# Down projections of two squared-ReLU MLPs as Strassen's seven products, with TensorE's instructions of both MLPs in source order

## The chip, the cores and the metric

The kernel runs on one core of one Trainium2 chip. The metric is the device time of one launch in microseconds; the time before is 1177.26 us, the median of three runs (1177.13 to 1177.45). A profile is one further execution, recorded by the hardware profiler. The engines are PE (TensorE: matmuls; PEld is its weight load), DVE (VectorE), ACT (ScalarE), POOL (GpSimd) and SP (which only issues transfers). ACT and SP issue the transfers from HBM on queues of their own. Each engine works through its instructions in order and waits on semaphores for the others.

## The reference

One inference step of a two-layer streaming encoder on 512 new and 64 running tokens, all in float32 (T = 576, model width D = 1024, inner width 4 D).

```
for i in range(2):
    x = x + mixer_i(rmsnorm(x, norm_mix[i]))      # 0: pooling mixer, 1: indexed sparse attention
    h = rmsnorm(x, norm_mlp[i])
    u = relu(h @ w_up[i])                         # 1024 -> 4096
    x = x + (u * u) @ w_down[i]                   # 4096 -> 1024
y = rmsnorm(x, norm_final)
```

The mixers also return new states (keys, values, indexer keys, the last 15 rows). The two MLPs hold most of the arithmetic: each has an up and a down product of 576 x 1024 x 4096.

## The kernel before, in words

The residual stream lies transposed in SBUF: eight feature tiles `x[k]` of 128 partitions by 576 tokens, two to a buffer. A float32 product is made from three matmuls in the fast float32 format: a value v is split into an upper part (ACT casts it) and a lower part (v less the upper part, a DVE subtraction), and upper x upper, upper x lower and lower x upper are summed in PSUM. `project` (L151 to L162) does this for one 128-wide output tile: eight k tiles, three passes, two halves of 288 tokens in two PSUM banks, so 48 matmuls.

Weights come in blocks of 128 x 1024 floats (512 KB): one output tile with its eight k tiles. `next_block` (L135) loads the next block by a transfer on ACT's queue, casts it on ACT (L115), subtracts on DVE (L116; on POOL at a few places) and keeps two blocks ahead. There are two raw buffers and three buffers each for the upper and lower parts.

`mlp` (L245) works in four chunks of 1024 inner features. A chunk is eight up products (`up`), each followed by relu and the factor 1/rms on DVE (L252), a square on ACT (L253) and a split into u (L145, L146); then eight down products (`dn`), each over the eight u tiles of the chunk and added into x[m] by DVE (L277). `xs` are the normalised inputs, split once; `Norm` sums squares of x, and `stats` and `spread` turn them into 1/rms on PE, ACT and DVE (the tiles `st` and `rb`). The first up product runs before 1/rms is known. The last three down products of layer 1 are made in two parts of the tokens by `last`, together with the final norm.

The order on each engine is set by a scheduler that goes by priorities and estimated times; it may move instructions of one stage between those of another. Only `last` holds PE to the source order, by `tc.manual_schedule`. All stages share the same pools of SBUF buffers; the MLPs borrow the tags of the attention for u and xs. PSUM has three slots of two banks (`ps`) and two of one bank (`po`).

Of the kernel before, what the change touches and what calls it, by code (L numbers as in the profile page):

```python
# [16 lines left out]
P = 128  # L17
# [19 lines left out]
SLOTS = {"x": 4, "xs": 8, "a": 3, "b": 3, "c": 3, "d": 3, "e": 2}  # L37
# [3 lines left out]
def pool_dsa_kernel(ctx: ExitStack, tc: tile.TileContext, a, o):  # L41
# [4 lines left out]
    slots = ctx.enter_context(tc.tile_pool(name="slots", bufs=1))  # L46
    weights = ctx.enter_context(tc.tile_pool(name="weights", bufs=3))
    raws = ctx.enter_context(tc.tile_pool(name="raws", bufs=2))
    tmps = ctx.enter_context(tc.tile_pool(name="tmps", bufs=4))
# [10 lines left out]

    def slot(tag, s, dt=F32R):
        return slots.tile([P, SLOT], dt, tag=tag, bufs=SLOTS[tag], name=uid(s))

# [3 lines left out]
    def tmp(s="t", tag="tmp", bufs=6):  # L67
        return tmps.tile([P, T], F32, tag=tag, bufs=bufs, name=uid(s))
# [16 lines left out]
    def const(shape, name, dt=F32):  # L85
        return cst.tile(shape, dt, tag=name, name=name)

# [8 lines left out]
    class Residual:  # L96
        """The residual stream: the feature tiles k as x[k], [P, T] each."""
# [7 lines left out]
    x = Residual()  # L105

# [5 lines left out]
    def split_weights(raw, n, top, sub):  # L112
        h = weights.tile([P, 4 * 264], F32R, tag="wh", name=uid("wh"))
        l = weights.tile([P, 4 * 264], F32R, tag="wl", name=uid("wl"))
        (act.copy if top is act else top.tensor_copy)(h[:, :n], raw[:, :n])  # L115
        sub.tensor_tensor(l[:, :n], raw[:, :n], f32(h[:, :n]), ALU.subtract)  # L116
        return h, l

    blocks = []

    def mlp_blocks(layer):
        for c in range(4):
            blocks.extend((a["w_up"][layer, c * 8 + f], KT * P) for f in range(8))
            blocks.extend((a["w_down"][layer, c, m], KT * P) for m in range(KT))

    mlp_blocks(0)
    blocks.extend((a["w_in"][j], KT * P) for j in range(5))
    blocks.extend((a["w_v"][j], 4 * 264) for j in range(2))
    blocks.extend((a["w_in"][j], KT * P) for j in range(5, 15))
    for _ in range(2):  # L130
        blocks.extend((a["w_o"][m], KT * P) for m in range(KT))
    mlp_blocks(1)
    split_blocks = []

    def next_block(ahead=2, queue=act, top=act, sub=dve):  # L135
        """The next block of weights in the order of use; those after it are on their way."""
        while blocks and len(split_blocks) <= ahead:
            src, n = blocks.pop(0)
            split_blocks.append(split_weights(load(src, n, queue), n, top, sub))
        return split_blocks.pop(0)  # L140

    def split(dst, src, scale=None, sub=dve):
        """dst [.., 2, n] takes the upper and lower parts of src (times scale)."""
        if scale is None:
            act.copy(dst[:, 0], src)  # L145
            sub.tensor_tensor(dst[:, 1], src, f32(dst[:, 0]), ALU.subtract)  # L146
        else:
            act.activation(dst[:, 0], src, AF.Copy, scale=scale)
            dve.scalar_tensor_tensor(dst[:, 1], src, scale, f32(dst[:, 0]), ALU.mult, ALU.subtract)

    def project(pt, w, xs, between=iter(()), cols=((0, HT), (HT, HT))):  # L151
        """pt[c, t] = sum over the k tiles of w[k, c] * xs[k, t], in three passes."""
        wh, wl = w
        n = len(xs)
        for k in range(n):
            next(between, None)
            for i, (wt, part) in enumerate(((wh, 0), (wh, 1), (wl, 0))):
                for h, (c, m) in enumerate(cols):
                    pe.matmul(  # L159
                        pt[:, h, :m], wt[:, k * P:(k + 1) * P], xs[k][:, part, c:c + m],  # L160
# [3 lines left out]
    class Norm:  # L164
        """1/rms of every token: by token on partitions as r, [P, 5], and along the free axis as rb, [P, T]."""
# [27 lines left out]
    def diagonals(r, n=T):  # L193
        """ident times column i of r, side by side."""
# [50 lines left out]
    def mlp(layer, gi, x_tags, u_tags, add=dve, end=None):  # L245
        norm = Norm(f"m{layer}")
        xs = split_x(gi, norm, x_tags, add)
        made = [0]

        def squared(pt):  # L250
            v = tmp("v")
            dve.scalar_tensor_tensor(halves(v), pt[:, :, :HT], 0.0, halves(norm.rb), ALU.max, ALU.mult)  # L252
            act.activation(v, v, AF.Square)  # L253
            u = pair_slot(u_tags[made[0] % len(u_tags)], "u")
            made[0] += 1
            split(u, v)
            return u

        for ch in range(4):
            us = []  # L260
            for f in range(8):
                w = next_block(sub=add if ch == 0 and f < 2 else dve)
                pt = psum("up")
                project(pt, w, xs)
                if ch == 0 and f == 0:
                    first = pt
                    norm.stats()
                    continue
                if ch == 0 and f == 1:
                    norm.spread()  # L270
                    us.append(squared(first))
                us.append(squared(pt))
            for m in range(KT if end is None or ch < 3 else KT - LAST):
                w = next_block()
                pt = psum("dn")
                project(pt, w, us)
                dve.tensor_tensor(halves(x[m]), halves(x[m]), pt[:, :, :HT], ALU.add)  # L277
        if end:
            end(us)

    def last(us):
        """The last products in two parts of the tokens, so that the final norm of one runs beside the other's."""
# [28 lines left out]
        def during(steps):  # L311
            """The steps of the first part's norm at their places among the second part's products."""
# [27 lines left out]
    def pool_mixer():  # L340
        """The groups' products first, z = (x gain) w with tokens on partitions, where 1/rms comes in;
        then z times bands: the mean over the window less the token itself. The last tile of z holds
        the sample's tokens and, from row TS, those of the state, which have their norm and gain."""
# [3 lines left out]
        def scratch(s, dt=F32):  # L347
            return tmps.tile([P, T], dt, tag="rp", bufs=4, name=s)
# [63 lines left out]
        def weights_upper(j):  # L412
            w[j] = [weights.tile([P, 4 * 264], F32R, tag=t, name=uid(t))[:, :KT * P] for t in ("wh", "wl")]
            act.copy(w[j][0], w_raw[j][:, :KT * P])

        def weights_lower(j, eng):
            eng.tensor_tensor(w[j][1], w_raw[j][:, :KT * P], f32(w[j][0]), ALU.subtract)
# [11 lines left out]
        def products(s, i):  # L429
            n = P if i < 4 else rows  # L430
            for g in range(2 * s, 2 * s + 2):
                for kk in range(2):
                    k = 2 * g + kk
                    c = (2 * (g % 2) + kk) * 256
                    wh, wl = (t[:, c:c + 256] for t in w[s])
# [30 lines left out]
        with tc.manual_schedule(engines={ENG.Activation, ENG.DVE, ENG.Pool}):  # L466
# [66 lines left out]
            src, n = blocks.pop(0)  # L533
            split_blocks.append(split_weights(load(src, n, act), n, act, pool))
# [39 lines left out]
        # the new state  # L574
# [9 lines left out]
    def attention():  # L584
# [6 lines left out]
        cs, sn = const([P, T], "cs"), const([P, T], "sn")  # L591
        nc.sync.dma_start(cs, a["cos"])
        nc.sync.dma_start(sn, a["sin"])
        V = const([P, 9, 256], "V")
        wi = const([P, 5, 8], "wi")
        nc.sync.dma_start(V[:, 4:8], a["cache_v"])

        # indexer keys: their halves twice over, [1, 2, 2, 1]
# [21 lines left out]
        def split_cache(src, s, new, sub=dve):  # L620
            """The cache's part of the sample's keys, with the new ones behind them."""
# [430 lines left out]
```

## Time and profile before

| | |
|---|---|
| median of three runs | 1177.26 us (1177.13 to 1177.45) |
| span of the profiled execution | 1175.3 us |
| PE busy | 1143.3 us (97%) |
| DVE, ACT, POOL busy | 595.4, 437.1, 169.1 us |
| mean granted TensorE clock | 0.988 |
| matmuls of the up and of the down products | 3072 each |
| a chunk of down products | 384 matmuls in 50.96 us |
| HBM traffic | 99.73 MB read, 13.25 MB written |

The page gives the profiled execution's span, from its first to its last instruction; the time of the launch around it is known only from the runs, whose median is 2.0 us longer. In the page a group's row ends with its busy time, the mean of one instruction in ns, and the idle time of its engine just ahead of it with what ended that idle time. The chain that ended last is followed back from the last instruction, and gives for each piece its start, its length and what was running. Windows give the busy time of each engine in a stretch. Matmuls are pipelined, so that the length of one (296 ns) is longer than the distance between two (133 ns).

### The profile page before, as it was taken

To read this page: it belongs to the slowest core of one execution; us is meant where nothing else is said; L and a number is where in the kernel's file an instruction comes from. 1 tells how busy PE (TensorE), PEld (TensorE's weight loads), DVE (VectorE), ACT (ScalarE), POOL (GpSimd) and SP (SyncE) were. 2 spreads that over 40 slices of the span, in tenths; PEclk is the share of its full clock that TensorE was granted. 3 is DMA by queue.
4 is the path that set the end of the run, shared out by engine and by line. 5 is a ranking of instruction groups with operands and counts; after the bars stand their busy time and mean duration, and the time that the engine had idled before them with its cause. 6 is when DMAs were issued, how large, how long until landed. Compare 5 with 4: busy or idle time off the path is not lost.

```text
span 1175.3 us, 20225 instructions
## 1 busy us (share of the span) xinstructions
PE 1143.3 (97%) x8580; PEld 1130.9 (96%) x8580; DVE 595.4 (51%) x1000; ACT 437.1 (37%) x713; POOL 169.1 (14%) x125
## 2 busy tenths in 40 slices
PE   7999999999999999998889999999999999999996
PEld 6999999999999999998879999999999999999995
DVE  7844234333333445869999943753343334324444
ACT  5633123123212433344377665542133123213331
POOL 7600000000000000227874430000000000000002
PEclk8999999999999999999989999999999999999998
DMA  6222222222222233456452341422322222222212
GB/s 208 60 90 72 90 84 79 91 74 89 87 76 90 75 128 121 149 175 185 144 159 75 119 126 45 150 74 89 87 76 91 76 87 90 73 90 80 84 55 81
DMA packets 51146, 116.64 MB, mean 99 GB/s; under 512 B 9345, under 2 KB 22960, under 8 KB 51056
## 3 DMA queue, kind: packets, MB, share of 16 engines
q10 hardware_dynamic: 23184, 84.45, 23.2%
q1 hardware_dynamic: 27872, 30.90, 8.6%
q8 instruction: 67, 1.10, 0.4%
q14 instruction: 23, 0.19, 0.0%
HBM read 99.73 MB, written 13.25 MB: 96 GB/s over the span
## 4 chain that ended last, share of the span: by engine, by line
PE 90%; DVE 6%; ACT 1%; issue 1%; DMA 1%; SPq 0%; DVEq 0%; ACTq 0%
PE up L159 35%; PE dn L159 34%; PE pj L159 5%; PE o L798 2%; PE wa L159 2%; PE wo L159 2%; DVE work L723 1%; PE sc L759 1%; PE pt L779 1%; PE v L915 1%; PE pb L548 1%; DVE m L722 1%; DVE wl L116 1%; PE o L802 1%; PE z L441 1%
## 5 line engine op out<-in xcount | busy, mean ns | idle before, releaser
L115 ACT CAST wh<-raw 128x1024 fp32r<-128x1024 f32 (+1 forms) x161 | 168.8, 1049 | 603.9 <-PE dn L159 299.3
L159 PE MATMUL dn<-u,wh 128*128 128x288 f32 (+2 forms) x2048 | 358.2, 296 | 0.0
L159 PE MATMUL up<-xs,wh 128*128 128x288 f32 x2048 | 356.3, 296 | 0.0
L159 PEld LDWEIGHTS dn<-u,wh 128*128 128x128 f32 x2048 | 301.3, 188 | 0.2
L159 PEld LDWEIGHTS up<-xs,wh 128*128 128x128 f32 x2048 | 300.1, 188 | 0.2
L159 PE MATMUL dn<-u,wl 128*128 128x288 f32 (+2 forms) x1024 | 222.9, 295 | 0.0
L159 PE MATMUL up<-xs,wl 128*128 128x288 f32 x1024 | 219.0, 295 | 0.0
L116 DVE TENSOR_TENSOR wl<-raw,wh 128x1024 fp32r<-128x1024 f32 (+1 forms) x149 | 186.3, 1250 | 30.4 <-ACT wh L115 23.0
L277 DVE TENSOR_TENSOR x<-x,dn 128x576 f32<-128x576 f32 x61 | 46.0, 754 | 245.5 <-PE dn L159 245.5
L159 PEld LDWEIGHTS dn<-u,wl 128*128 128x128 f32 x1024 | 165.8, 188 | 0.0
L159 PEld LDWEIGHTS up<-xs,wl 128*128 128x128 f32 x1024 | 164.4, 188 | 0.1
L252 DVE SCALAR_TENSOR_TENSOR v<-up,rbm 128x576 f32<-128x576 f32 x64 | 48.3, 757 | 204.9 <-PE up L159 204.3
L159 PE MATMUL pj<-xs,wh 128*128 128x288 f32 x448 | 79.5, 296 | 0.0
L305 POOL TENSOR_TENSOR x<-x,rb 128x320 f32<-128x320 f32 (+1 forms) x9 | 7.9, 908 | 454.7 <-ACT rb L301 454.7
L159 PEld LDWEIGHTS pj<-xs,wh 128*128 128x128 f32 x448 | 66.5, 188 | 0.6
L606 POOL TENSOR_TENSOR cs<-cs,rba 128x576 f32<-128x576 f32 x1 | 1.9, 1862 | 415.2 <-ACT rba L190 415.2
L146 DVE TENSOR_TENSOR u<-v,u 128x576 fp32r<-128x576 f32 x64 | 48.4, 758 | 13.3 <-ACT u L145 13.2
L159 PE MATMUL pj<-xs,wl 128*128 128x288 f32 x224 | 48.4, 295 | 0.0
L738 ACT ACTIVATE p<-p,nm 128x128 f32<-128x128 f32 (+4 forms) x72 | 41.9, 584 | 10.4 <-DVE nm L737 10.1
L253 ACT ACTIVATE v<-v 128x576 f32<-128x576 f32 x64 | 43.9, 687 | 2.4 <-DVE v L252 1.9
L145 ACT CAST u<-v 128x576 fp32r<-128x576 f32 x64 | 43.1, 676 | 1.9
L798 PEld LDWEIGHTS o<-V,pT 128*128 128x128 f32 x320 | 40.2, 196 | 1.9 <-ACT pT L780 1.5
(191 smaller groups left out, 1215.4 us busy)
## 6 DMA issues: line engine op xcount, KB each, us to landing
raw<-in_w_up ACTq DMA_DIRECT2D x64, 512.0 KB, 3.6
raw<-in_w_down ACTq DMA_DIRECT2D x64, 512.0 KB, 3.5
raw<-in_w_o ACTq DMA_DIRECT2D x16, 512.0 KB, 3.6
raw<-in_w_in ACTq DMA_DIRECT2D x15, 512.0 KB, 3.9
q<-st SPq DMA_DIRECT2D x32, 144.0 KB, 2.5
q<-q SPq DMA_DIRECT2D x16, 256.0 KB, 2.8
x<-in_x SPq DMA_DIRECT2D x8, 288.0 KB, 5.9
xd<-x SPq DMA_DIRECT2D x4, 576.0 KB, 2.8
```

The lines of the kernel that those rows point to most:

```text
L115: (act.copy if top is act else top.tensor_copy)(h[:, :n], raw[:, :n])
L116: sub.tensor_tensor(l[:, :n], raw[:, :n], f32(h[:, :n]), ALU.subtract)
L145: act.copy(dst[:, 0], src)
L146: sub.tensor_tensor(dst[:, 1], src, f32(dst[:, 0]), ALU.subtract)
L159: pe.matmul(pt[:, h, :m], wt[:, k * P:(k + 1) * P], xs[k][:, part, c:c + m], start=(k == 0 and i == 0), stop=(k == n - 1 and i == 2),)
L252: dve.scalar_tensor_tensor(halves(v), pt[:, :, :HT], 0.0, halves(norm.rb), ALU.max, ALU.mult)
L253: act.activation(v, v, AF.Square)
L277: dve.tensor_tensor(halves(x[m]), halves(x[m]), pt[:, :, :HT], ALU.add)
L441: pe.matmul(z[s, i][:n, (g % 2) * 256:(g % 2 + 1) * 256], lhs, rhs, start=kk + j == 0, stop=kk == 1 and j == 2)
L548: pe.matmul(pt[:, c0:c0 + rhs.shape[1]], lhs, rhs, start=n == 0, stop=n == len(steps) - 1)
L738: act.activation(dst, dst, AF.Exp, scale=-1.0, bias=nm, accum_out=sums)
L798: pe.matmul(oc[:, 2 * s + hh], pT[:, c:c + P], V[:, kt, vs], start=kt == 0, stop=kt == i)
```

## The change

Four things change together.

First, the down products of all four chunks of layer 0 and of the first three chunks of layer 1 are made by Strassen's scheme in its form with seven products. A pair of output tiles (2q, 2q+1), the two halves of a chunk's eight k tiles, and the two halves of the tokens give 2 x 2 blocks. Instead of eight block products there are seven, each of four k tiles, three passes and 288 tokens (12 matmuls). For this, seven weight factors are made for each pair (a11, a12, a21 + a11, a22 and three sums; four sums of 128 x 512 on POOL), and seven activation factors from each pair of u tiles (f, f + 4), by `factors`. `Pair` keeps three PSUM banks a, b and c: `opening` makes three products and adds them to x or to the common sum g (ACT copies g in the first chunk, DVE adds to it later); `closing` makes four more, which go on accumulating in the same banks, each followed by a DVE update of half of an x tile. b is used twice in `closing` (t3, then t4), so that the update after t3 has to be done before t4 starts. In the last Strassen chunk POOL adds g to three halves of the pair's x tiles. The last chunk of layer 1 has plain down products as before.

Second, weights are split in units of 128 x 512 (half a block, or a factor) instead of whole blocks, with six buffers, and one unit in four in two more buffers during the MLPs. `next_unit` keeps four units ahead, `next_block` takes two units. The two raw tiles of a pair (512 KB each) come from a pool of two buffers, and its sums from a pool of four.

Third, PE's instructions of both MLPs are held to the source order. In the source the first up product of the next chunk comes before the down products of this one, and the up products come in the order 0, 4, 1, 5, 2, 6, 3, 7. `stats` stands right behind the first up product and `spread` behind the second. The attention's instructions are still placed by the scheduler, also between those of the last pair of layer 0's MLP.

Fourth, each stage has buffer pools of its own that are released at its end; only x, the constants, the weights, the raw blocks and two norm buffers live through.

The new functions and the core of the diff (line numbers of the changed kernel: split 166/167, POOL sums 186 to 194, factors 337 to 349, product 351 to 357, Pair 359 to 396):

```
+            r = [phase["pairs"].tile([P, KT * P], F32, tag="pair", bufs=2, ...) for _ in range(2)]
+            for t, src in zip(r, (one, two)):
+                act.dma_start(t, src)
+            a11, a12, a21, a22 = (t[:, i * 512:(i + 1) * 512] for t in r for i in range(2))
+            s1, s2 = (phase["pairs"].tile([P, 512], F32, tag="sum", bufs=4, ...) for _ in range(2))
+            pool.tensor_tensor(s1, a21, a22, ALU.add)
+            pool.tensor_tensor(s2, s1, a11, ALU.add)
+            yield split_unit(a11)
+            yield split_unit(s2)
+            yield split_unit(s1)
+            pool.tensor_tensor(a21, a21, a11, ALU.add)
+            yield split_unit(a12)
+            yield split_unit(a21)
+            pool.tensor_tensor(s2, s2, a12, ALU.add)
+            yield split_unit(s2)
+            yield split_unit(a22)
...
+        def factors(v):
+            t = phase["acts"].tile([P, 4, HT], F32, tag="t", bufs=1, name=uid("t"))
+            u = phase["u"].tile([P, 7, 2, HT], F32R, tag="u", bufs=4, name=uid("u"))
+            b12, b11, b22, b21 = (v[:, i] for i in range(4))
+            act.copy(u[:, 0:3, 0], v[:, 1:4])
+            dve.tensor_tensor(t[:, 0], b11, b12, ALU.subtract)
+            dve.tensor_tensor(t[:, 1], b22, t[:, 0], ALU.add)
+            dve.tensor_tensor(t[:, 2], b12, b22, ALU.subtract)
+            dve.tensor_tensor(t[:, 3], b21, t[:, 1], ALU.subtract)
+            act.copy(u[:, 3:7, 0], t)
+            dve.tensor_tensor(u[:, 0:3, 1], v[:, 1:4], f32(u[:, 0:3, 0]), ALU.subtract)
+            dve.tensor_tensor(u[:, 3:7, 1], t, f32(u[:, 3:7, 0]), ALU.subtract)
+            return u
...
+        def product(bank, w, us, factor, js, first, last):
+            for j in js:
+                wh, wl = (t[:, j * P:(j + 1) * P] for t in w)
+                uh, ul = (us[j][:, FACTORS.index(factor), i] for i in range(2))
+                for i, (wt, ut) in enumerate(((wh, uh), (wh, ul), (wl, uh))):
+                    pe.matmul(bank[:, :HT], wt, ut, ...)
...
+            def opening(self, parts=((0, 1, 2, 3),)):
+                ws = [next_unit() for _ in range(3)]
+                for js in parts:
+                    for w, bank, factor in zip(ws, (self.a, self.b, self.c_), ("b11", "t2", "t1")):
+                        product(bank, w, self.us, factor, js, True, True)
+                    yield
+                self.opened()
+            def opened(self):
+                q = self.q
+                if self.c == 0:
+                    part_sums[q] = phase["acts"].tile([P, HT], F32, tag=f"g{q}", bufs=1, name=uid("g"))
+                    act.copy(part_sums[q], self.a[:, :HT])
+                else:
+                    dve.tensor_tensor(part_sums[q], part_sums[q], self.a[:, :HT], ALU.add)
+                dve.tensor_tensor(self.hi[0], self.hi[0], self.b[:, :HT], ALU.subtract)
+                dve.tensor_tensor(self.hi[1], self.hi[1], self.c_[:, :HT], ALU.subtract)
+                if self.c == strassen - 1:
+                    g = part_sums[q]
+                    pool.tensor_tensor(self.hi[0], self.hi[0], g, ALU.add)
+                    pool.tensor_tensor(self.hi[1], self.hi[1], g, ALU.subtract)
+                    pool.tensor_tensor(self.lo[1], self.lo[1], g, ALU.subtract)
+            def closing(self):
+                js = (0, 1, 2, 3)
+                for bank, factor, out, b2 in ((self.a, "b21", self.lo[0], 0), (self.b, "t3", self.hi[1], 0),
+                                              (self.c_, "b22", self.hi[0], 0), (self.b, "t4", self.lo[1], 0)):
+                    product(bank, next_unit(), self.us, factor, js, False, True)
+                    dve.tensor_tensor(out, out, bank[:, :HT], ALU.add)
...
-    pool_mixer()
-    mlp(0, 1, ["xs"] * KT, "abcdabcdabcd", pool)
-    attention()
-    mlp(1, 3, "aaabbbcc", ["xs"] * KT + ["c", "d", "d", "d"], end=last)
+    with stage(slots=1, xs=1, tmps=6):
+        pool_mixer()
+    with stage(u=1, xs=1, acts=1, tmps=3, pairs=1, more=2):
+        with tc.manual_schedule(engines={ENG.PE}):
+            mlp(0, 1, 4, pool)
+    with stage(slots=1, xs=1, cst2=1, tmps=6):
+        attention()
+    with stage(xs=1, u=1, acts=1, tmps=3, pairs=1, more=2):
+        with tc.manual_schedule(engines={ENG.PE}):
+            mlp(1, 3, 3, end=last)
```

More of the change, by code (lines that the diff above doesn't have):

```diff
@@ L110, in load @@
         return raw
[L112 to L116, printed above, removed]
-        return h, l
[L119 to L140, printed above, removed]
+    jobs = []
@@ L142, in split, with next_unit, next_block, at @@
+    units = made()
+    def next_unit(ahead=4, sub=dve):
+        how["sub"] = sub
+        while len(ready) <= ahead:
+            u = next(units, None)
+            if u is None:
+                break
+            ready.append(u)
+        return ready.pop(0)
+    def next_block(sub=dve):
+        return [next_unit(5 - i, sub) for i in range(2)]
+    def at(w, k):
+        return [t[:, (k % 4) * P:(k % 4 + 1) * P] for t in w[k // 4]]
     def split(dst, src, scale=None, sub=dve):
@@ L532, in pool_mixer @@
             dve.tensor_copy(sband, sraw)
-            src, n = blocks.pop(0)
-            split_blocks.append(split_weights(load(src, n, act), n, act, pool))
+            how["sub"] = pool
+            for _ in range(2):
+                ready.append(next(units))
         two = psum("z")
@@ L677, in attention @@
                 nc.sync.dma_start(f32(qis[-1][:, 4 * j:4 * j + 4]), qi[j][:, :, i * P:i * P + np_])
-        work = [None] + [const([P, (i + 1) * P if i < 4 else TP + TS], f"work{i}") for i in range(1, 5)]
+        work = [None] + [const([P, (i + 1) * P if i < 4 else TP + TS], f"work{i}", pool=cst) for i in range(1, 5)]
         def index_scores(i):
```

190 lines of the change are left out of this document (143 added, 47 removed).

## The prediction

> **What bounds the kernel now.** I read the page's busy shares first, then the chain that ended last in order of time, then busy time by stage (windows), then the groups of instructions kept apart by shape.
>
> ```profile
> span 1175.3 us, 20225 instructions
> PE 1143.3 (97%) x8580; PEld 1130.9 (96%) x8580; DVE 595.4 (51%) x1000; ACT 437.1 (37%) x713; POOL 169.1 (14%) x125
> ```
>
> ```profile
> 101.84 50.96 PE dn L159 x384
> 152.80 51.01 PE up L159 x384
> ...
> 458.68 6.39 PE ki L159 x48
> 465.19 0.99 PE st L209 x10
> 466.19 6.46 PE pj L159 x47
> 472.64 0.97 PE rb L189 x4
> 473.62 19.11 PE pj L159 x144
> ...
> 636.55 2.85 PE wa L159 x24
> ```
>
> ```profile
> 15.00:25.00 10.00, 5.92 (x42) 5.50 (x40) 9.18 (x16) 2.09 (x4) 9.54 (x10) 0.84 0.32 117
> 25.00:33.00 8.00, 8.00 (x55) 7.99 (x55) 7.08 (x22) 7.79 (x16) 1.59 (x1) 0.77 0.37 132
> 101.80:152.80 51.00, 51.00 (x387) 51.00 (x386) 16.60 (x17) 9.79 (x11) 0.00 (x0) 1.00 0.27 83
> ```
>
> The columns of the windows are length, then busy time (count) of PE, PEld, DVE, ACT and POOL, then clock, DMA share and GB/s. Both MLPs are PE work without a gap: a chunk of down products is 384 matmuls in 50.96 us, 132.7 ns each, at clock 1.00, while DVE is busy 16.6 us of 51 and POOL not at all. So a matmul less is 132.7 ns less, as long as the other engines keep up. Those matmuls alternate between two PSUM banks; the new products stay in one bank for twelve. The output product of the attention does that too: 24 matmuls, 256 wide, in 2.85 us, 119 ns each, and 119 x 288/256 is 133.6 at most. I take 132.7.
>
> The profiled span is 1175.3 us, the median 1177.26 us; I take the 2.0 us outside the span as unchanged and make the sum against 1177.3.
>
> **The gain.** Per chunk, 4 pairs x 7 products x 4 k tiles x 3 passes = 336 matmuls instead of 384. Seven chunks change (all four of layer 0, three of layer 1): 336 matmuls fewer, 336 x 132.7 ns = **44.6 us**. A product is 12 matmuls, 1.59 us, a pair 84, 11.15 us, and each pair saves one product: what a pair loses to waits must stay below 1.59 us.
>
> **What it adds, beside PE.** The rows for the prices:
>
> ```profile
> raw<-in_w_down ACTq DMA_DIRECT2D x64, 512.0 KB, 3.5
> ```
>
> ```profile
> L116 DVE TENSOR_TENSOR wl<-raw,wh 128x1024 fp32r<-128x1024 f32 x147 | 183.8, 1250 | 30.4 <-ACT wh L115 23.0
> L146 POOL TENSOR_TENSOR ck<-raw,ck 128x512 fp32r<-128x512 f32 x4 | 5.2, 1293 | 12.6 <-ACT ck L145 6.6 <-issue 6.0
> L946 POOL TENSOR_TENSOR x<-x,wo 128x256 f32<-128x256 f32 x8 | 5.7, 731 | 11.8 <-DMA x<-xd 11.8
> L145 ACT CAST ck<-raw 128x512 fp32r<-128x512 f32 x4 | 2.5, 622 | 2.2 <-DMA raw<-in_cache_k 2.2
> L843 DVE TENSOR_TENSOR ot<-ot,ot 128x128 fp32r<-128x128 f32 x32 | 7.6, 279 | 0.7 <-ACT ot L841 0.7
> L827 DVE TENSOR_TENSOR on<-o,rs 128x256 f32<-128x256 f32 x16 | 6.5, 408 | 1.8 <-PE o L798 1.8
> ```
>
> The two small DVE rows give 129 ns per 128 columns and 150 ns fixed: 288 columns 0.44 us, 512 columns 0.66 us. Per pair: seven units of 512 columns, so seven casts on ACT (0.62) and seven subtractions on DVE (0.65), 4.3 and 4.6 us; six or seven 288-wide updates of x and g on DVE, 2.9 us; four 512-wide sums on POOL, 5.2 us. All of it is below the pair's 11.15 us, so none costs anything by its amount. The activation factors of an up pair (three passes of 288 after the first, then subtractions of 864 and 1152 columns on DVE, two casts on ACT) are about 4 us of DVE in 12.7 us of PE; the first up product of the next chunk (6.4 us) and three quarters of the opening stand between the last factors and their use. I cost them at nothing; without that cover each chunk would pay about 5 us.
>
> What is not hidden is a chain of waits. A pair's two raw tiles have two buffers, so the second raw of the next pair is loaded only when the last unit (a22) of this one is split, and POOL's sums wait for it. By the order of the instructions on DVE, from the end of one pair's a22 subtraction to the next pair's: load 3.5, two POOL sums 2.6, cast 0.62, then on DVE subtraction, update, two subtractions, update 2.85 (here the last product, t4, may start, since it accumulates in the bank this update reads), then subtraction, update, subtraction 1.75: 11.3 us. The pair is 11.15. With nothing in its way this chain costs 0.15 us a turn. Behind the load's wait on ACT's queue stand the next pair's casts, which need that load or the one before it anyway; behind each update on DVE stands the next subtraction, so a late unit delays the update behind it, and the update delays PE. SP issues nothing in these stretches; the loads of the weights are as many and as large as before.
>
> But DVE subtractions and POOL sums disturb each other:
>
> ```profile
> 575.81 1.43 POOL L650 TENSOR_TENSOR rp<-rp,sn 128x576 f32<-128x576 f32 x1
> 576.54 1.77 DVE L116 TENSOR_TENSOR wl<-raw,wh 128x1024 fp32r<-128x1024 f32 x1
> 577.19 2.42 POOL L649 TENSOR_TENSOR rp<-rp,cs 128x576 f32<-128x576 f32 x1
> ```
>
> ```profile
> 474.13 1.86 POOL L606 TENSOR_TENSOR cs<-cs,rba 128x576 f32<-128x576 f32 x1 [415.25 <-ACT rba L190]
> 474.63 1.98 DVE L607 TENSOR_TENSOR sn<-sn,rba 128x576 f32<-128x576 f32 x1
> ```
>
> A DVE subtraction of 1.25 took 1.77 and the POOL operation under it 2.42 instead of 1.43. For half the columns: DVE +0.3, POOL +0.5. In a turn three subtractions meet POOL's third and fourth sums, and one POOL sum on the chain is met: +1.4, so 12.7, **1.55 us late a turn**. There are two turns in a chunk (pair 1 to 2, 2 to 3; the first pair is prepared under the up products, the last is followed by whole blocks), less half a us in hand at the start: 2.6 us a chunk. Ends: 0 (no meeting) and 4.5 (all as in the second fence, and the first pair late too). I take 2.6, as the first fence is the same subtraction. Three plain chunks: **7.8**.
>
> First chunk of each layer: ACT copies g out of bank a, and stands behind two casts that wait for POOL's sums of pair 1. That pair's second raw is issued about 1.4 us before the down products begin: load to 2.1, sums to 4.7, casts to 6.0, copy to 6.4. PE wants the bank after 36 matmuls, 4.8. So 1.6 more: 4.2 each, **8.4** (ends 0 and 6).
>
> Last Strassen chunk of each layer: three 288-wide POOL adds a pair (0.8 by the 256-wide row), two of them between the two sums of the next pair: +1.6 a turn, 3.2. Layer 1: **5.8**. In layer 0, ACT also scales and squares x for the attention ahead of the load: **6.6**. Ends 2 and 9.
>
> From layer 0's MLP to the attention. In the changed order PE runs the first three projections, then the statistics (st), then rb, with nothing between, and the fourth projection needs a PSUM slot that only the rotated keys free:
>
> ```profile
> 468.61 0.25 DVE L202 TENSOR_SCALAR diag<-ident,r 128x64 f32<-128x64 f32 x1
> ...
> 477.31 0.76 DVE L610 TENSOR_TENSOR t<-ki,sn 64x576 f32<-64x576 f32 x1
> ```
>
> From st (465.19) to the end of diag 3.7, from rb (472.64) to the end of that product 5.4: 9.1, of which 1.5 is st and rb themselves. In the run shown the second projection and the next ones cover all of it; now it is bare: **8** (7.6 and something for the squares, which now stand behind casts on ACT, and whose last sums wait on DVE behind a subtraction of a block not yet loaded). Ends 3 and 12.
>
> The granted clock was 0.84 in a stretch with PE busy 5.92 of 10 us and 0.77 in the full 8 us behind it, so a long stall costs some 1.8 us more behind it; that lies inside the upper end. [...]
>
> Start of each MLP. PE's fixed order puts st after 48 matmuls, not 60:
>
> ```profile
> 48.69 8.01 PE up L159 x60
> 56.70 0.99 PE st L209 x10
> ```
>
> Twelve matmuls are 1.6 us; in layer 0 DVE also has two subtractions ahead of the last sums of squares, and POOL the first pair's sums among its own: **2** and 0.5 in layer 1 (ends 0 and 4). The halved blocks in the attention: two casts and two subtractions instead of one of each, 0.07 us of DVE each; on the chain for a few blocks, **0.5**.
>
> Sum: 1177.3 - 44.6 + 7.8 + 8.4 + 5.8 + 6.6 + 8 + 2.5 + 0.5 = **1172.3**.
>
> **The rivals.** *The queues keep up.* DVE is idle two thirds of a down chunk, and 11.3 against 11.15 needs only a little luck. Then only the boundary and the ends of the layers are paid, about 3 + 4 + 2: 1142. Against it: the meetings of DVE and POOL are in the trace. 0.17.
>
> *Slower: the load-and-sum chain is the bound in every pair.* It decides when the down phases lose more than 44.6 - 11 = 33.6 us, 1.2 us over each of 28 pairs. At the upper ends of the terms above (3 x 4.5 + 2 x 6 + 9 + 9, 43.5) with 11 for the rest: 1187. For it: DVE in the second fence made next to no headway until POOL was done (1.98 for 0.75). 0.36.
>
> [...]
>
> *The change does not do what it says*, PE at more than 132.7 ns in one bank: excluded within 1 ns by the 24 matmuls above; no chance of its own.
>
> **How the numbers follow.** Within 0.2% (2.4 us), which is what this kernel's measurement can tell from nothing, ends the middle case at its slow side: 0.12. The middle case faster (1145 to 1174.9) 0.35, the queues keeping up 0.17, slower 0.36. So faster 0.52, same 0.12, slower 0.36. The range runs from the first rival to a little past the second, 1142 to 1192; the middle case by itself is 1155 to 1176.
>
> **What would show it.** PE with 336 matmuls fewer; a quiet pair at 11.15 us; idle PE before the seventh product of pairs 1 and 2 of a chunk, released by DVE's update of x, and none in pair 3; POOL's sums and DVE's subtractions longer than 1.3 and 0.66; PE idle 5 to 10 us behind rb in the attention. It is wrong if the gaps sit elsewhere (the up products, the factors), if loads take longer than 3.5 us, or if pairs run without gaps.

## The result, and the profile after

The changed kernel takes 1250.4 us (median of four runs, 1248.0 to 1253.1), against 1177.4 us before: 1.062 times as long, 95% interval 1.0598 to 1.0642. The forecast was 1172, with a range of 1142 to 1192. One execution each of two kernels further down, 2757 us of "both" and 2859 us of "without Strassen", lies far outside the others of its kernel, and the times given for these two are medians of the others. The profiled execution has a span of 1250.0 us. From its page:

```profile
span 1250.0 us, 20624 instructions
PE 1132.7 (91%) x8244; PEld 1109.9 (89%) x8244; DVE 827.6 (66%) x1478; ACT 534.1 (43%) x968; POOL 351.7 (28%) x274
...
L356 PE MATMUL ab<-u,wh 128*128 128x288 f32 x1120 | 242.3, 310 | 68.6 <-DVE x L396 50.2
...
L356 PE MATMUL c<-u,wh 128*128 128x288 f32 x448 | 93.5, 301 | 0.0
```

PE has 336 instructions fewer (8580 to 8244), as the change says, and its busy share has fallen from 97% to 91%. The third line is the finding: ahead of the products in banks a and b PE was idle for 68.6 us, most of it until a DVE update of x from a bank had ended (L396); ahead of those in c not at all. The rest of the 68.6 us ended with the update from b behind the opening (L383, 10.4 us), with late weights (ACT's cast L166, 4.1) and with late activation factors (3.9). Windows over eight stretches tell where: first the start of layer 0's MLP, then six Strassen chunks, and behind the dots a chunk of up products. Columns as in the prediction's windows: length, busy time and count of PE, PEld, DVE, ACT and POOL, then the granted clock, DMA share and GB/s.

```profile
47.66:74.07 26.41, 18.46 (x115) 17.99 (x114) 10.89 (x18) 7.92 (x15) 12.67 (x8) 0.81 0.17 58
118.36:177.16 58.80, 48.73 (x340) 47.44 (x339) 36.53 (x53) 18.88 (x34) 20.63 (x15) 0.94 0.27 84
228.00:281.70 53.70, 45.72 (x339) 44.64 (x338) 36.60 (x57) 17.33 (x30) 20.88 (x15) 1.00 0.30 91
332.53:387.69 55.16, 47.27 (x339) 46.17 (x338) 36.85 (x57) 17.34 (x30) 20.94 (x15) 0.97 0.28 87
859.76:920.56 60.80, 50.05 (x339) 48.78 (x338) 37.44 (x53) 18.91 (x34) 21.33 (x15) 0.92 0.26 78
971.33:1030.30 58.97, 48.74 (x339) 47.66 (x338) 38.05 (x57) 17.52 (x30) 21.28 (x15) 0.94 0.26 81
1081.10:1138.90 57.80, 47.98 (x338) 46.24 (x338) 36.86 (x56) 18.10 (x31) 29.72 (x24) 0.97 0.20 65
...
177.16:228.00 50.84, 50.84 (x387) 50.84 (x386) 32.38 (x47) 22.87 (x32) 1.30 (x1) 1.00 0.23 72
```

The up products run as before, 50.84 us without a gap, although DVE now is busy 32 of 51 us there. Each of these six Strassen chunks takes 53.7 to 60.8 us: with 48 matmuls fewer each is longer than the 50.96 of a plain chunk. Against 44.6 (336 x 132.7 ns) they lose 77.7 us together. The seventh, the last of layer 0, goes from 432.2 to 502.6 and holds 54 matmuls of the attention (7.2 us): 63.2, a loss of 18.6. So the chunks lose 96.3 us, where the forecast had 28.6. The rest by stretches: the start of layer 0's MLP, first up product to the end of rb, went from 15.4 to 26.4 us (+11), that of layer 1's from 15.7 to 18.6 (+3), the attention, with the 7.2 us of it that ran earlier, from 291.5 to 301.2 (+9.7). Then -44.6 + 96.3 + 11 + 3 + 9.7 = 75.4; the spans differ by 74.7.

One of the waits, in the timeline of the second pair of the first chunk (start, length, engine, line, and in brackets the idle time and its releaser):

```profile
141.35 1.23 DVE L167 TENSOR_TENSOR wl<-pair,wh 128x512 fp32r<-128x512 f32 x1
...
142.09 0.29 PE L356 MATMUL ab<-u,wl 128*128 128x288 f32 x1
142.72 1.54 DVE L167 TENSOR_TENSOR wl<-sum,wh 128x512 fp32r<-128x512 f32 x1
...
144.18 0.44 DVE L396 TENSOR_TENSOR x<-x,ab 128x288 f32<-128x288 f32 x1
144.34 1.27 POOL L194 TENSOR_TENSOR sum<-sum,pair 128x512 f32<-128x512 f32 x1 [0.63 <-DVE wl L167]
...
144.68 0.85 PE L356 MATMUL ab<-u,wh 128*128 128x288 f32 x2 [2.30 <-DVE x L396]
...
145.56 0.68 PE L356 MATMUL ab<-u,wh 128*128 128x288 f32 x2
...
147.72 0.45 PE L356 MATMUL c<-u,wh 128*128 128x288 f32 x2
```

The product b21 in bank a ends at 142.4. Its update of x (L396) stands on DVE behind the subtractions of two weight units of the next pair, drawn out from 0.69 to 1.23 and 1.54 beside POOL's sums, and ends at 144.6. Only then does PE start, and what it starts is t3, which goes into bank b. Nothing in t3 needs what that update reads. Its twelve matmuls then take 3.04 us, to 147.72, instead of 1.59: after the wait they come 0.24 us apart instead of 0.13. The granted clock is 0.50 over these twelve (144.68 to 147.72) and 0.94 over the chunk.

Two theories came from this. **S**, shared tile: a and b are the two banks of one tile `ab`, and the wait is kept for the tile; a product in b waits until DVE has read a. **L**, loads and sums, the forecast's own mechanism: the second raw tile of the next pair comes late, POOL's sums behind it, and so DVE's updates stand behind late subtractions. They can both hold: S makes PE wait for the update, L makes the update late.

The same place shows in the whole trace. Of the 28 pairs 27 have a wait ahead of t3, 25 of them ended by the update L396 (0.55 to 4.47 us) and two by a late cast of weights. Ahead of t4, where the forecast had the waits, there are only four, all in the last Strassen chunk of a layer (0.74, 3.06, 0.74 and 3.09 us).

### The profile page after: what moved, and what is told of

It reads as the page before. It is cut to its first block, busy times and chain, and to the rows that moved or that the text cites. A ratio compares the mean times of both kernels' runs of the same rounds, so it can differ in the third digit from the quotient of the medians.

```text
span 1250.0 us, 20624 instructions
## 1 busy us (share of the span) xinstructions
PE 1132.7 (91%) x8244; PEld 1109.9 (89%) x8244; DVE 827.6 (66%) x1478; ACT 534.1 (43%) x968; POOL 351.7 (28%) x274
## 4 chain that ended last, share of the span: by engine, by line
PE 61%; issue 14%; DVE 13%; POOL 6%; ACT 3%; DMA 2%; SPq 0%; DVEq 0%; ACTq 0%; POOLq 0%
PE up L234 30%; PE ab L356 8%; DVE wl L167 4%; PE dn L234 4%; PE pj L234 3%; PE c L356 3%; PE o L971 2%; PE wo L234 2%; PE wa L234 2%; DVE work L896 2%; POOL sum L187 2%; DMA pair<-in_w_down 1%; DVE m L895 1%; POOL sum L186 1%; PE v L1088 1%
## 5 line engine op out<-in xcount | busy, mean ns | idle before, releaser
L356 PE MATMUL ab<-u,wh 128*128 128x288 f32 x1120 | 242.3, 310 | 68.6 <-DVE x L396 50.2
L356 PEld LDWEIGHTS ab<-u,wh 128*128 128x128 f32 x1120 | 188.8, 198 | 78.4 <-DVE x L396 32.9
L166 ACT CAST wh<-raw 128x512 fp32r<-128x512 f32 (+1 forms) x210 | 128.7, 620 | 237.7 <-PE up L234 102.9
L167 DVE TENSOR_TENSOR wl<-raw,wh 128x512 fp32r<-128x512 f32 (+1 forms) x186 | 148.4, 801 | 74.2 <-ACT wh L166 72.8
L356 PE MATMUL ab<-u,wl 128*128 128x288 f32 x560 | 171.6, 306 | 0.0
L166 ACT CAST wh<-sum 128x512 fp32r<-128x512 f32 x84 | 50.9, 619 | 163.9 <-PE ab L356 49.7
L167 DVE TENSOR_TENSOR wl<-pair,wh 128x512 fp32r<-128x512 f32 x112 | 96.3, 864 | 29.9 <-ACT wh L166 28.5
L166 ACT CAST wh<-pair 128x512 fp32r<-128x512 f32 x112 | 69.1, 619 | 107.8 <-PE up L234 40.8
L356 PEld LDWEIGHTS ab<-u,wl 128*128 128x128 f32 x560 | 111.5, 199 | 0.0
L356 PE MATMUL c<-u,wh 128*128 128x288 f32 x448 | 93.5, 301 | 0.0
L167 DVE TENSOR_TENSOR wl<-sum,wh 128x512 fp32r<-128x512 f32 x84 | 75.0, 898 | 21.6 <-ACT wh L166 19.7
L356 PEld LDWEIGHTS c<-u,wh 128*128 128x128 f32 x448 | 74.8, 196 | 0.0
```

Source lines behind the costliest of these rows:

```text
L166: act.copy(h, src)
L167: how["sub"].tensor_tensor(l, src, f32(h), ALU.subtract)
L356: pe.matmul(bank[:, :HT], wt, ut, start=first and j == 0 and i == 0, stop=last and j == 3 and i == 2, skip_group_check=True)
```

## The experiments

**The banks.** a and c share a tile, b has its own, so that no two products in succession write the same tile.

```
-                ab = psum("ab")
-                self.a, self.b, self.c_ = ab[:, 0], ab[:, 1], psum1("c")
+                ac = psum("ac")
+                self.a, self.b, self.c_ = ac[:, 0], psum1("b"), ac[:, 1]
...
-                    for w, bank, factor in zip(ws, (self.a, self.b, self.c_), ("b11", "t2", "t1")):
+                    for i, bank, factor in ((0, self.a, "b11"), (2, self.c_, "t1"), (1, self.b, "t2")):
+                        w = ws[i]
```

The update from c (L384) is put ahead of that from b. 

> The order of the pairs' PSUM banks alone: a and c share a tile of two banks, b has a tile of its own, and the opening makes a, c, b instead of a, b, c; so no two products that follow each other write the same tile. Theory S (shared tile): in the changed kernel PE waits ahead of the fifth product (t3, bank b) of nearly every pair until DVE has read bank a, only because a and b are one tile. Then the 0.5 us waits vanish, the longer ones shrink by up to one product, 1.59 us; the waits of the seven Strassen chunks, 68 us, come down to about 23, and the matmuls at a lower clock behind them, some 29 us, to about 10: 1187 us (1178 to 1202). Theory L (loads and sums): the next pair's raw tile comes late, DVE's updates stand behind its late subtractions, and the bound is this chain, whatever the banks: 1235 us (1228 to 1245), with the same 2 us waits one product further on.

Measured: 1201.4 us, 1.020 times the kernel before (1.0179 to 1.0221), 49 us less than the changed kernel. The page's groups:

```profile
L356 PE MATMUL ac<-u,wh 128*128 128x288 f32 x896 | 186.1, 301 | 19.7 <-DVE x L384 9.5
...
L356 PE MATMUL b<-u,wh 128*128 128x288 f32 x672 | 139.7, 300 | 10.4 <-DVE x L397 9.7
```

The waits fell from 68.6 to 30.1 us; S had said about 23, and 1187. The time lies at the upper edge of the range that S was given (1178 to 1202): S holds, a little oversized; L alone, 1235, is out. Where the changed kernel waits, PE now goes on in bank b while DVE reads bank a:

```profile
127.62 0.68 PE L356 MATMUL b<-u,wh 128*128 128x288 f32 x2
127.86 0.46 DVE L397 TENSOR_TENSOR x<-x,ac 128x288 f32<-128x288 f32 x1 [1.24 <-PE ac L356]
```

Of the waits that are left, 9.7 us ahead of products in b are for the update of b itself, as the forecast had them; 9.5 and 6.3 us ahead of products in a and c end with updates from these two, which again share a tile.

**The loads.** Each of a pair's two raw tiles gets a second buffer: the second one uses the two buffers of the blocks, which the pairs left unused.

```
-            r = [phase["pairs"].tile([P, KT * P], F32, tag="pair", bufs=2, name=uid("pair")) for _ in range(2)]
+            r = [phase["pairs"].tile([P, KT * P], F32, tag="pair", bufs=2, name=uid("pair")),
+                 raws.tile([P, 4 * 264], F32, tag="raw", name=uid("raw"))[:, :KT * P]]
```

> The raw tiles alone: a pair's second raw tile comes from the two buffers of the blocks, so that each of the two tiles of a pair has a second buffer, and the loads of the next pair need not wait for the last unit of this one. Theory L: POOL's sums start 4 us earlier or more, no update stands behind a late subtraction, and of the waits only the 0.55 us of the shared tile are left, 28 of them with 2 us for the first pairs, 17 us: 1195 us (1185 to 1210). Theory S: the wait ahead of the fifth product is for the update of bank a and stays in every pair; DVE's queue has the same subtractions in it: 1240 us (1230 to 1250).

Measured: 1215.9 us, 1.032 times (1.0300 to 1.0348), 34.5 us less than the changed kernel.

```profile
L357 PE MATMUL ab<-u,wh 128*128 128x288 f32 x1120 | 239.1, 307 | 45.9 <-DVE x L397 25.7
```

It lies between the two figures, in neither range. 3.8 of the 34.5 us are gained at the start of layer 0's MLP, the rest in the chunks. 45.9 us of waits are left, and in most pairs the one ahead of t3 is now 0.55 to 0.65 us: that is DVE's update with nothing in its way (0.45, and the start behind the last matmul and the release), the least that the shared tile costs here. So L is at work too, and S sets a floor under it.

**Both.** 

> Both edits. If only S is right, as with the banks alone, 1187 us, within 6 us of it. If only L, as with the loads alone, 1195, within 6 us. If both are at work and each hides what the other leaves, the pairs run at nearly 11.15 us, 10 to 20 us below the better of the two: 1172 us (1160 to 1185).

Measured: 1179.6 us, 1.0016 times (1.0003 to 1.0030), 71 us less than the changed kernel, within the range for both at work; the two alone add up to 83.5, so they overlap by 13.

```profile
L357 PE MATMUL ac<-u,wh 128*128 128x288 f32 x896 | 186.8, 302 | 18.4 <-DVE x L385 12.3
...
L357 PE MATMUL b<-u,wh 128*128 128x288 f32 x672 | 138.6, 299 | 4.1 <-DVE x L398 3.9
```

```profile
114.13:165.56 51.43, 46.56 (x336) 45.86 (x336) 34.37 (x53) 18.85 (x33) 13.13 (x9) 0.97 0.30 92
216.54:262.40 45.86, 44.79 (x337) 44.33 (x336) 34.81 (x57) 17.69 (x29) 12.87 (x9) 1.00 0.33 104
820.35:872.17 51.82, 46.62 (x336) 45.92 (x336) 33.70 (x52) 18.56 (x33) 12.46 (x9) 0.97 0.30 91
```

The second chunk of layer 0 takes 45.86 us, 1.3 above the ideal 44.6, at clock 1.00. The first chunk of each layer still takes 51.4 and 51.8.

**The control to the banks.** The order of the products and updates as with the banks, but a and b in one tile again.

```
-                ac = psum("ac")
-                self.a, self.b, self.c_ = ac[:, 0], psum1("b"), ac[:, 1]
+                ab = psum("ab")
+                self.a, self.b, self.c_ = ab[:, 0], ab[:, 1], psum1("c")
```

> The control to the banks: the same order of products and updates as there (opening a, c, b), but a and b share the tile again and c stands alone; raw tiles as in the changed kernel. Theory S (it is the shared tile that makes PE wait): the products on a after b, on b after a follow each other in one tile, PE waits for DVE's update twice in every pair, at least 0.5 us each time, and the time is that of the changed kernel or more: 1250 us and up (1245 to 1275). If the order of the products made the gain of the banks: 1201 us (1195 to 1208).

Measured: 1289.0 us, 1.093 times (1.0899 to 1.0967).

```profile
L356 PE MATMUL ab<-u,wh 128*128 128x288 f32 x1120 | 249.3, 316 | 89.6 <-DVE x L397 42.0
```

The same order of work is 88 us slower by the grouping of the banks alone, and now PE waits in most pairs for two updates, 89.6 us together with the few other waits (42.0 ended by the updates of `closing`, 40.7 by that from b behind the opening, 0.91 us at least). That shows S: it is the tile and not the order. The wait of b for a reader of a is nothing that the memory asked for in these two runs: as shown above, the kernel with the banks regrouped writes bank b, from 127.62 on, while DVE reads a, for 0.46 us from 127.86 on.

**Without the sums.** POOL's four sums per pair are left out, and the seven units are split straight from the quarters of the raw tiles.

```
-            pool.tensor_tensor(s1, a21, a22, ALU.add)
-            pool.tensor_tensor(s2, s1, a11, ALU.add)
             yield split_unit(a11)
-            yield split_unit(s2)
-            yield split_unit(s1)
-            pool.tensor_tensor(a21, a21, a11, ALU.add)
+            yield split_unit(a22)
+            yield split_unit(a21)
...
```

> The changed kernel without POOL's four sums of weights in each pair: the seven units are split straight from the quarters of the two raw tiles (so the products are of other factors; loads, casts, subtractions and matmuls are as many and as large). Banks and raw tiles as in the changed kernel. Theory L, with the sums as the late link: a turn loses 2.6 us of sums and the meetings of DVE and POOL, the second raw tile has only a cast behind it, and what is left are the waits of the shared tile: 1205 us (1195 to 1220), about as with the earlier loads, and the waits at the start of layer 0's MLP shrink. If the load is the late link by itself, 3.5 us behind the last unit of the pair before, whatever comes behind it: 1235 us (1225 to 1250).

Measured: 1201.3 us, 1.021 times (1.0181 to 1.0235): 49 us less than the changed kernel, with its shared tile and its two raw buffers.

```profile
L351 PE MATMUL ab<-u,wh 128*128 128x288 f32 x1120 | 231.4, 300 | 38.4 <-DVE x L391 30.6
```

So of L the sums, with their meetings with DVE's subtractions, weigh more than the load: without them the waits are 38.4 us, with earlier loads 45.9, and in both runs 3.8 us are gained at the start of layer 0's MLP. The two are links of one chain, so their gains do not add up.

**Without Strassen.** All down products plain, everything else as changed.

```
-    mlp_jobs(0, 4)
+    mlp_jobs(0, 0)
...
-            mlp(0, 1, 4, pool)
+            mlp(0, 1, 0, pool)
```

(and layer 1 likewise). 

> All that changed except Strassen: the down products of all chunks are plain (48 matmuls each, eight products), with the half-block units, TensorE's source order in both MLPs and the stages' own pools as in the changed kernel. By the stretches of the two traces the changed kernel loses 11 us at the start of layer 0's MLP, about 11 in and around the attention and 3 at the start of layer 1's MLP. If these come from the units, the source order and the stages: 1202 us (1195 to 1208), and chunks of 51 us without a gap. If POOL's sums for the first pair make most of the loss at the start, 8 less: 1194 us. If the source order itself costs time within the chunks, above 1210 us.

Measured: 1183.6 us, 1.0048 times (1.0033 to 1.0062), below all three figures. Half-block units, source order and stages cost 6 us together, not 25. For its profile it ran once more. 

> Once more the kernel without Strassen (all else as changed), for its profile. It took 6 us more than the kernel before. If the new place of the statistics costs them: a wait ahead of st in layer 0's MLP of about 3 us and a lower clock behind it, and chunks of 51 us without a wait; if the attention does: waits around rb there, as in the changed kernel.

It took 1184.1 us. PE's timeline at the start of layer 0's MLP:

```profile
59.36 0.80 PE L284 MATMUL st<-ones,s 128*128 128x2 f32 x3 [5.84 <-DVE s L252]
```

The loss is here: a wait of 5.84 us ahead of the statistics, and matmuls further apart behind it (three of the statistics' in 0.80 us, where PE's timeline of the kernel before has ten in 1.15); from the first up product to the end of rb it is 25.2 us instead of 15.4, with a start 2.2 us earlier. The plain chunks take 50.8 us each, and the attention starts as in the kernel before (first projection, st, second projection, rb) with no wait around rb; so units, source order and stages alone do not make what the changed kernel loses there. At the start they make most of it, 9.8 of 11 us. The timelines of the kernel before and of the changed kernel:

```profile
41.78 9.16 POOL L177 TENSOR_TENSOR s<-s,sq 128x576 f32<-128x576 f32 x5
```

```profile
47.36 5.83 POOL L252 TENSOR_TENSOR s<-s,sq 128x576 f32<-128x576 f32 x3 [3.54 <-ACT sq L251]
53.16 1.72 POOL L186 TENSOR_TENSOR sum<-pair 128x512 f32<-128x512 f32 x1
54.85 1.84 POOL L252 TENSOR_TENSOR s<-s,sq 128x576 f32<-128x576 f32 x1
56.65 1.26 POOL L187 TENSOR_TENSOR sum<-sum,pair 128x512 f32<-128x512 f32 x1
57.88 1.26 POOL L191 TENSOR_TENSOR pair<-pair,pair 128x512 f32<-128x512 f32 x1
59.09 1.39 POOL L252 TENSOR_TENSOR s<-s,sq 128x576 f32<-128x576 f32 x1
...
62.20 2.17 PE L284 MATMUL st<-ones,s 128*128 128x2 f32 x10 [7.95 <-DVE s L252]
```

POOL starts its five sums of squares 5.6 us later than before, since ACT's squares come later, and three sums of the first pair of weights, 4.2 us, stand among them. Without these sums the wait was 4.26 us (the run before this one). With the earlier loads it was 4.29: there the sums come too, but behind the five squares. So it is their place among the squares that costs, 3.7 us.

**Steps.** On top of both edits, g is copied by DVE, and the statistics and the spreading of 1/rms come one up product later.

```
-                    act.copy(part_sums[q], self.a[:, :HT])
+                    dve.tensor_copy(part_sums[q], self.a[:, :HT])
...
-                if n == 0:
+                if n == 1:
                     norm.stats()
+                if n < 2:
                     continue
-                if n == 1:
+                if n == 2:
                     norm.spread()
```

> The kernel with both edits (banks and loads), and two steps more: g is copied out of bank a by DVE instead of ACT, and the statistics stand behind the second up product of each MLP and the spreading of 1/rms behind the third, one product later each. With both edits, the first Strassen chunk of each layer still takes 51.4 and 51.8 us, the later ones 45.9 to 47.4; there ACT's copy stands behind casts that wait for POOL's sums. If that place of the copy is the cause (theory C), both first chunks come down to about 46, 11 us less; if the late load of the second pair alone is (theory L), they stay above 50. The wait of 4.28 us ahead of the statistics and the matmuls at a lower clock behind it go: 6 us. C: 1163 us (1157 to 1169); L: 1174.

Measured: 1166.6 us, 0.991 times the kernel before (0.9895 to 0.9930). The first chunks:

```profile
109.61:155.60 45.99, 44.80 (x336) 44.33 (x336) 35.00 (x57) 17.63 (x29) 12.83 (x9) 1.00 0.34 103
810.89:857.81 46.92, 45.01 (x337) 44.34 (x337) 34.70 (x57) 17.54 (x29) 12.59 (x9) 1.00 0.33 101
```

They take 5.4 and 4.9 us less than with both edits alone: C holds. The wait ahead of the statistics is gone; a wait of 1.3 us behind rb is left.

**Plain last chunk in layer 0**, and then **no source order for it**: `mlp_jobs(0, 3)` and `mlp(0, 1, 3, pool)` in place of 4; then the source order of layer 0 ends ahead of that chunk's down products. 

> The one before, with plain down products in the last chunk of layer 0 too (Strassen in three chunks of each layer). With both edits that chunk took 56.6 us without the projections between its products, more than the 51 of a plain chunk: waits of 3.3 and 1.0 us for the last pair's activation factors, with no up product behind them, and 2.8 in the third pair. If the loss is the chunk's own: 5 us less than the one before. If the loss moves on to the start of the attention, where the statistics of x are late in any case: no less.

Measured: 1160.6 us, 0.986 times (0.9848 to 0.9881), 6 less than with the steps; the chunk takes 51.0 us. The loss was the chunk's own. 

> The one before, with TensorE's source order in layer 0 given up ahead of the last chunk's down products, so that the scheduler may place the first projections of the attention as in the kernel before. If the source order up to the end of the MLP makes the waits around rb in the attention (2.7 and 4.1 us, and a lower clock behind them): 8 us less than the one before. If they come from the late statistics, or from PSUM slots: the same within 3 us.

Measured: 1159.3 us, 0.986 times (0.9841 to 0.9876), 1.3 less than the one before: the same. The waits in the attention stand, in PE's timeline:

```profile
467.11 1.24 PE L265 MATMUL rb<-diag,ones 128*128 128x288 f32 x4 [2.70 <-DVE diag L275]
472.45 1.33 PE L235 MATMUL pj<-xs,wh 128*128 128x288 f32 x4 [4.11 <-DVE t L791]
```

So the source order of this last stretch is not what makes them. In this kernel too three projections run ahead of the statistics, and in the kernel without Strassen one does; why the scheduler turns them round was not settled. With the one before it, it is the fastest of all kernels here, faster than both that were compared, 17 us below the kernel before.

| kernel | us | waits ahead of products in a, b (and c) | ratio to before |
|---|---|---|---|
| before | 1177 | | 1 |
| changed | 1250.4 | 68.6 | 1.062 |
| banks | 1201.4 | 30.1 | 1.020 |
| loads | 1215.9 | 45.9 | 1.032 |
| both | 1179.6 | 22.5 | 1.002 |
| control | 1289.0 | 90.0 | 1.093 |
| without sums | 1201.3 | 38.4 | 1.021 |
| without Strassen | 1183.6 | | 1.005 |
| both, steps | 1166.6 | 15.1 | 0.991 |
| both, steps, plain last chunk | 1160.6 | 8.6 | 0.986 |
| both, steps, plain last chunk, no source order for it | 1159.3 | 8.9 | 0.986 |

The waits are the idle times of the groups of the pairs' products (for the control with 0.4 us ahead of c). From the changed kernel to the banks 38.5 us of waits take 49 us of time with them, to the loads 22.7 take 30.7 (34.5 without the 3.8 at the start), from the changed kernel to the control 21.4 bring 39: a microsecond of wait costs 1.3 to 1.8. The matmuls behind some of the waits run slower, as at 144.68 above; that this is all of the difference was not shown.

## Why the prediction was wrong, point by point

**The step that failed** is in the chain of waits: "here the last product, t4, may start, since it accumulates in the bank this update reads". It let each product wait for its own bank alone. PE in fact waited two products earlier, ahead of t3, for the update of the other bank of the same tile, in 27 of 28 pairs, the last of a chunk included, where the forecast had none; in the chunks that are not the last of a layer no t4 waited. The six chunks outside the end of layer 0 lost 77.7 us, where the forecast had 22.0 (7.8 + 8.4 + 5.8). `ab = psum("ab")` with `ab[:, 0], ab[:, 1]` stands in the diff; that one tile means one wait was not asked. With three banks that wait only for their own readers, an update has the time of one or two products to be late, 1.6 to 3.2 us by 1.59 a product, and, as an estimate, most of the lateness would have stayed hidden (with the banks regrouped as above, 30.1 of the 68.6 us of waits were left); with the shared tile it has none. Banks against control, 1201 against 1289 with the same order of work, shows that the tile makes the wait.

**The chain of load and sums** was there, in place and direction: raw tile, sums, cast, subtraction, late update, DVE and POOL drawing each other out (a unit's subtraction 0.69 alone, 1.2 to 1.8 when met). Its term, 2.6 us a plain chunk from two turns, was mis-sized: it assumed that only the lateness beyond a pair's 11.15 us reaches PE. Earlier loads brought 34.5 us, leaving the sums out 49, 3.8 of each at the start of layer 0's MLP.

**The clock** was put "inside the upper end". It is a term of its own. In the six chunks the waits make 56.7 us of the 77.7 lost; the granted clock (0.94, 1.00, 0.97, 0.92, 0.94, 0.97 over those lengths) accounts for some 15 of the other 21, an estimate by length times what is missing to 1.

**First chunks**: the forecast had ACT's copy of g behind two casts that wait for POOL, 1.6 us late. The place was right, the wait was 3.9 and 2.6 us. In the first of them the copy ended at 125.90, 2.6 us after PE could have gone on; the rest is DVE's update from b (L383), which came behind the copy and two subtractions, to 127.17, and for which the product in a waited too, the tile being one. On top of both edits, moving the copy to DVE, together with the later statistics, which stand ahead of these chunks, took 5.4 and 4.9 us from them.

**Last chunk of layer 0**: 6.6 us forecast, 18.6 measured. Of its 11.9 us of waits 8.0 are ended by updates, as in the other chunks. The rest, the activation factors, was costed at nothing with its cover named, the first up product of the next chunk; in the last chunk there is none, and PE waited 3.3 and 0.5 us for the last pair's factors (L347, L348). That the cover was gone just there was overlooked.

**Start of layer 0's MLP**: 2 us forecast, 11 measured. The statistics at the earlier place were costed by the twelve matmuls that no longer cover them alone; that POOL would start its sums of squares 5.6 us later was not looked for; its three sums of weights among them, named without a price, were 4.2 us; and the clock fell to 0.81 in this stretch.

**Right**: 336 matmuls fewer; the up products without a gap and the activation factors hidden under them in the other chunks; 132.7 ns a matmul in one bank (with both edits a chunk of 336 takes 45.9 us with about 1 us of idle time in it); and the attention, 8.5 us forecast and 9.7 measured, with waits where they were said to be, 2.17 us ahead of rb and 4.11 behind it, and 1.87 ahead of the statistics.

**The rival that came closest** was the slower one: a chain that bounds every pair, deciding from 1.2 us over in each. The chunks were 96.3 / 28 = 3.4 us over in each. Its price of 1187 was the sum of the terms' upper ends, and the ends of the chunk terms were set for waits of one bank at full clock. The gain itself was no mistake: the last kernel, with Strassen in six chunks, 288 matmuls fewer or 38 us, and most of these waits gone, is 17 us below the kernel before.

## What to carry to other kernels

Before costing an accumulation that jumps between banks, look up which banks are one tile: here a product waited for the readers of the whole tile, so products in succession belong in different tiles (1201 us against 1289 in the same order), with a product's time, here 1.59 us, between a bank's update and the next write to its tile. An engine that both feeds PE and frees PE's banks in one queue, as DVE here, turns a late feed into a late release (the update at 144.18 stood behind subtractions of 1.23 and 1.54 us, and PE waited 2.30); give the feed a second buffer, which took 34.5 us off here, and keep sums that nothing waits for yet off the queue where something waits, 3.7 us here. Cost a row of short waits with the lower clock behind them, here 1.3 to 1.8 us of time for each microsecond of wait.

## What was not expected of the hardware

After the wait of 2.30 us shown above twelve matmuls took 3.04 us instead of 1.59, at a granted clock of 0.50; after another wait of 2.30 us, at 248.4, twelve took 1.66, about their usual pace (the granted clock is 1.00 over that whole chunk, whose longest wait this is):

```profile
250.70 0.50 PE L356 MATMUL ab<-u,wh 128*128 128x288 f32 x2 [2.30 <-DVE x L396]
251.03 0.29 PE L356 MATMUL ab<-u,wl 128*128 128x288 f32 x1
251.17 0.43 PE L356 MATMUL ab<-u,wh 128*128 128x288 f32 x2
```

The fourth matmul starts 0.47 us behind the first there, 0.88 us at 144.68. Behind the wait of 2.56 us at 867.08 the first six matmuls take 0.90 us, close to the usual pace, and those behind them come 0.24 us apart, at a granted clock of 0.50 from 867.98 to 872.97. The chunk with clock 0.92, which holds that wait, has none above 3.8 us. So the clock fell behind one wait of 2.30 us and not behind an equal one; what decides it these traces do not show.
